# A hybrid mLSTM and SSD layer: side work of ScalarE and VectorE queued behind the latest bank copy and bank sum

## The chip, the cores and the metric

The kernel runs on one core of a Trainium2 chip, as one program. The metric is device time in microseconds (us). In what follows PE is TensorE (the matmuls), DVE is VectorE, ACT is ScalarE, POOL is GpSimd, and SP is the queue that issues the DMAs.

## What is computed

One decoder layer on 2048 tokens of width 1024, all in float32. The normalised stream is multiplied by one wide input matrix; its columns feed four mLSTM heads and two SSD groups, which run as recurrences over chunks of 128 tokens; both results are gated, normalised, and mapped back by an output matrix. Cut to what matters:

```python
h = rms_norm(x, norm_w[l])
proj = h @ w_in[l]                       # 2048 x 1024 by 1024 x 6680
q, k, v, i_pre, f_pre, o_pre, z_m, z_s, xbc, dt_raw = jnp.split(proj, SPLIT_POINTS, axis=-1)
hm = mlstm_chunkwise(q, k, v, log_i, log_f)          # 4 heads, chunks of 128
hm = norm(hm) * sigmoid(o_pre) * silu(z_m)
xs, Bm, Cm = split(silu(causal_depthwise_conv(xbc)))
y = ssd_chunked(xs, dt, A, Bm, Cm) + d_skip * xs     # 2 groups of 8 heads, chunks of 128
y = norm(y * silu(z_s))
x = x + concatenate([hm, y]) @ w_out[l]
return rms_norm(x, final_norm_w)
```

## The kernel before

**Products.** Both large matrix products are cut into 68 jobs. A job makes two blocks of 128 rows by 1024 columns by a Strassen-like scheme of seven products (`strassen`). One product is 12 matmuls of 128x512, because each operand is split into a high and a low float32r part (`split`: a cast on ACT, L191, and a difference on DVE, L192) and three of the four combinations are used. The left operands of a job are named L11, L12, S2, S3, S1, S4, L22, the right ones, which stay in SBUF for many jobs, R11, R21, T2, T3, T1, R22, T4. So a matmul `pj<-R22h,S4h` belongs to the sixth product of its job.

**Banks.** Products L11, S2, S1 and S4 add into the same PSUM bank `pa`, and between two of them ACT copies the bank out (*bank copy*: lines 276, 283, 289, and 302 or 327 for the last). The next product into the bank must wait for that copy. Two further banks are added to what was copied by DVE (*bank sum*: lines 280, 290, 296). Between the third copy (L289) and the product S4 only one product of the next job, L12, stands on PE. What a copy writes (`oa`, `ob`, `ca`, `cbt`) is one of four buffers, which comes free when the store of an earlier job's result (to `hd` or `gd`) has landed.

**Side work.** After each product `step` is called. It prepares the left operands of a coming job by one notch (`left`), and then lets other work go on by small pieces: the recurrences of a finished head or group (`rec_head`, `rec_group`, paced by `wv.to`), what they postponed (`later`, run by `tick`), the gates of a block of tokens (`gates`), and the operands of a later stage (`next_h`, `next_w`, called *prepared operands*: loads `xt`, `we`, `wg`, scalings in L511 and L533, splits `hqh`, `hql` in L396 and L398, and stores to DRAM). In a head's recurrence `scores` makes, for a chunk, `E` and `w` from a row `nmi` that a DMA loads (`w` in L690, `E` in L686 on DVE and L688 on ACT), then `kw`, `vt` and `st`; `memory` uses them on PE one turn later (L714 to L718).

**What sets the order.** PE runs its instructions in the order in which the program is written (`manual_schedule`). On the other engines and on SP a scheduler sets the order, when the kernel is built: it goes by its own reckoning of when an instruction can start, and lets one that seems to be ready pass another that was written earlier. On the chip each of these engines then works through its list in that order, and an instruction that waits holds all behind it.

Of the kernel before, what the change touches and what calls it, by code (L numbers as in the profile page):

```python
# [12 lines left out]
AF = mybir.ActivationFunctionType  # L13
# [56 lines left out]
def hybrid_layer(ctx, tc, x, norm_w, w_in, b_igate, b_fgate, conv_w, conv_b, dt_bias,  # L70
                 a_log, d_skip, mlstm_norm_w, ssd_norm_w, w_out, final_norm_w, out):
    nc = tc.nc
# [11 lines left out]
    def pj_tile():  # L84
        return psp.tile([P, TB], F32, tag="pj", name="pj")
# [8 lines left out]
    def ot(nm, n=1024):  # L94
        return mk([P, SUP + 16], "o", 4, nm)[:, 0:n]
# [4 lines left out]
    def tt_(nm):  # L100
        return mk([P, 1024], "t", 1, nm)
# [79 lines left out]
    def tick(n=1):  # L181
        clock[0] += n
        for t, fn in list(due):
            if t <= clock[0]:
                due.remove((t, fn))
                fn()
# [78 lines left out]
    def product(ps, L, R, start):  # L265
        lh, ll = L
        rh, rl = R
        for k in range(4):
            for n, (l, r) in enumerate(((lh, rh), (lh, rl), (ll, rh))):
                nc.tensor.matmul(ps, lhsT=l[:, k, :], rhs=r[:, k, :], start=start and k + n == 0,  # L270
                                 stop=k == 3 and n == 2, skip_group_check=True)

    def strassen(L, R, oa, ob, copy):
        pa = pj_tile()
        product(pa, L["L11"], R["R11"], True)
        nc.scalar.copy(oa[0], pa)  # L276
        yield
        ps = pj_tile()
        product(ps, L["L12"], R["R21"], True)
        nc.vector.tensor_add(oa[0], ps, oa[0])  # L280
        yield
        product(pa, L["S2"], R["T2"], False)
        nc.scalar.copy(ob[0], pa)  # L283
        yield
        pd = pj_tile()
        product(pd, L["S3"], R["T3"], True)
        yield
        product(pa, L["S1"], R["T1"], False)
        nc.scalar.copy(ob[1], pa)  # L289
        nc.vector.tensor_add(ob[1], pd, ob[1])  # L290
        yield
        product(pa, L["S4"], R["R22"], False)
        copy(oa[1], pa)
        yield
        product(pd, L["L22"], R["T4"], False)
        nc.vector.tensor_add(ob[0], pd, ob[0])

    def halves(t, o=0):
        return t[:, o:o + TB], t[:, o + TB:o + SUP]

    def evac_copy(dst, ps):
        nc.scalar.copy(dst, ps)

    def pair(L, R, s, ph, kind, j):
        n = int(ph[1])
        if kind == "conv":
            a, b = ot("ca", SUP + 3), ot("cbt", SUP + 3)
            yield from strassen(L, R, halves(a, 3), halves(b, 3), evac_copy)
            for i, raw in enumerate((a, b)):
                t = (8 + 2 * i + n) if j == 0 else n * 4 + j - 2 + i  # L310
                nc.scalar.copy(raw[:, 0:3], halo[:, t, :])
                nc.scalar.copy(halo[:, t, :], raw[:, SUP:SUP + 3])
                dst = tt_("cd")
                nc.scalar.activation(dst, raw[:, 0:SUP], AF.Identity, scale=cw[:, t, 0:1],
                                     bias=cb[:, t:t + 1])
                for q in range(1, 4):
                    nc.vector.scalar_tensor_tensor(dst, raw[:, q:q + SUP], cw[:, t, q:q + 1], dst,
                                                   op0=ALU.mult, op1=ALU.add)
                nc.scalar.activation(raw[:, 0:SUP], dst, AF.Tanh)
                nc.vector.scalar_tensor_tensor(raw[:, 0:SUP], raw[:, 0:SUP], 1.0, dst, op0=ALU.add, op1=ALU.mult)  # L320
                nc.sync.dma_start(gd[s][n][:, j + i, :], raw[:, 0:SUP])
            yield
            return
        a, b = ot("oa"), ot("ob")
        if kind == "oz":
            def first(dst, ps):
                nc.scalar.activation(dst, ps, AF.Tanh, scale=0.5)

            yield from strassen(L, R, halves(a), halves(b), first)
            nc.scalar.activation(a[:, 0:TB], a[:, 0:TB], AF.Tanh, scale=0.5)  # L330
            t = tt_("tz")
            nc.scalar.activation(t, b, AF.Tanh, scale=0.5)
            nc.vector.scalar_tensor_tensor(b, a, 1.0, b, op0=ALU.add, op1=ALU.mult)
            nc.vector.scalar_tensor_tensor(b, t, 1.0, b, op0=ALU.add, op1=ALU.mult)
            nc.sync.dma_start(hd[s][n][:, 4 + j, :], b)
        elif kind == "raw":
            yield from strassen(L, R, halves(a), halves(b), evac_copy)
            nc.sync.dma_start(hd[s][n][:, j, :], a)
            nc.sync.dma_start(hd[s][n][:, j + 1, :], b)
        else:  # L340
            yield from strassen(L, R, halves(a), halves(b), evac_copy)
            for i, z in enumerate((a, b)):
                t = tt_("tz")
                nc.scalar.activation(t, z, AF.Tanh, scale=0.5)
                nc.vector.scalar_tensor_tensor(z, t, 1.0, z, op0=ALU.add, op1=ALU.mult)
                nc.sync.dma_start(gd[s][n][:, j + i, :], z)
        yield
# [36 lines left out]
    def right_tile(o):  # L384
        return tuple(mk([P, 4, TB], o + k, 1, o + k, F32R) for k in "hl")

    def refill(o, d):
        rt = right_tile(o)
        for i in range(2):
            nc.sync.dma_start(rt[i].bitcast(F32), d[o][:, i])  # L390
        return rt
# [601 lines left out]
    def left():  # L993

        if ahead[0] < len(order):
            next(jobs[order[ahead[0]]]["left"])
            ahead[0] += 1
# [7 lines left out]
    def step(n, o):  # L1005

        left()
        if n + 1 < len(jobs) and jobs[n + 1]["new"]:
            st = jobs[n + 1]["stage"]
            Rs[st][o] = refill(o, refs[st])  # L1010
        tick()
        for t in [k for k in plan if k <= clock[0]]:
            for g in plan.pop(t):
                next(g, None)
        wv.to()
# [18 lines left out]
    for n, jb in enumerate(jobs):  # L1034
# [15 lines left out]
        if n == 0:  # L1050
            next(g)
            next(first)
            next(gm0)
            next(first)
            left()
            left()
            step(n, "R21")
        more = n + 1 < len(jobs)
        next(g)
        step(n, "T2")  # L1060
        next(g)
        step(n, "T3")
        if more:
            begin(n + 1)
# [51 lines left out]
```

## Time and profile before

| | |
|---|---|
| median of 3 runs | 1823.45 us |
| lowest and highest | 1819.24 and 1826.52 us |
| profiled execution, its own time | 1829.99 us |
| its span, first to last instruction | 1828.2 us |
| mean granted TensorE clock in it | 0.966 of full speed |
| busy: PE, DVE, ACT, POOL | 92%, 72%, 48%, 25% of the span |
| DMA packets' time, as a share of the 16 engines' span | 68.1% |

The span is what the trace shows; the 1.8 us around it are the launch's. Busy time is an average over stages that differ, and PE's is modelled: a matmul counts as busy until its result is drained, so matmuls overlap and a busy PE may still lose time to a lower clock. What PE loses is read from the gaps before its matmuls, and from what ended each gap.

### The profile page before, as it was taken

The page shows a single profiled execution, that of the slowest core. Times are in us where ns is not written, and L with a number is a line of the kernel's source. Part 1 is how long each engine was busy: PE and PEld are TensorE (multiplying, and loading weights), DVE is VectorE, ACT ScalarE, POOL GpSimd, SP SyncE. Part 2 cuts the span into 40 slices and gives each one's busy share as a digit, 9 for nine tenths or more (in the row PEclk, how much of TensorE's full clock was granted, in tenths as well). Part 3 has the DMA queues.
Part 4 walks back from the last instruction along what each step waited for, and adds up shares of the span by engine and source line. Part 5 has one row for each costly group of instructions (what it writes and reads, how often), then busy time and mean ns, then how long its engine had stood idle before and what let it go on. Part 6 is the DMA issues. An engine that isn't in the chain of part 4 may idle for free.

```text
span 1828.2 us, 25057 instructions
## 1 busy us (share of the span) xinstructions
PE 1679.5 (92%) x8072; PEld 1357.2 (74%) x8072; DVE 1308.7 (72%) x2417; ACT 880.6 (48%) x1880; POOL 450.2 (25%) x629
## 2 busy tenths in 40 slices
PE   4999999999899798989899999898988889997997
PEld 4688887778788685767788777777776667776885
DVE  7677968877567693888675895655678578864775
ACT  5344644456566663434564444655565433332443
POOL 2000413332122131223121331202211144532222
PEclk9999999999999899999999999999999989998999
DMA  5245666668787689655575658888877976678543
GB/s 153 93 156 174 185 212 203 207 212 256 224 258 231 181 274 379 206 182 179 161 203 185 196 181 272 290 278 263 258 260 250 384 260 212 205 265 315 189 158 115
DMA packets 358323, 405.32 MB, mean 222 GB/s; under 512 B 30224, under 2 KB 284432, under 8 KB 352816
## 3 DMA queue, kind: packets, MB, share of 16 engines
q1 hardware_dynamic: 358192, 403.72, 68.1%
q8 instruction: 64, 1.05, 0.2%
q14 instruction: 67, 0.55, 0.1%
HBM read 251.40 MB, written 152.24 MB: 221 GB/s over the span
## 4 chain that ended last, share of the span: by engine, by line
PE 25%; DMA 15%; DVE 7%; issue 3%; ACT 2%; SPq 1%; POOL 1%; DVEq 0%; POOLq 0%; ACTq 0%
PE pj L270 21%; DMA E<-arow 1%; DMA we<-in_w_out 1%; DVE E L798 1%; DMA nmi<-mrow 1%; DMA mx<-mix 1%; DMA gin<-gd 1%; DMA ws1R<-hqh 1%; DMA T4l<-ws1T 1%; DMA ws0T<-hql 1%; DMA ws0R<-hqh 1%; DMA ws0T<-hqh 1%; DMA xr<-in_x 1%; DMA ws1T<-hqh 1%; PE rc L872 1%
## 5 line engine op out<-in xcount | busy, mean ns | idle before, releaser
L733 POOL TENSOR_SCALAR sq<-dn,sq 128x1 f32<-128x1 f32 x64 | 46.1, 720 | 624.9 <-ACT sj L731 477.8
L270 PE MATMUL pj<-R22h,S4h 128*128 128x512 f32 x272 | 119.7, 440 | 38.1 <-ACT ob L289 24.6
L270 PE MATMUL pj<-T2h,S2h 128*128 128x512 f32 x272 | 113.4, 417 | 11.6 <-ACT ca L276 9.3
L270 PE MATMUL pj<-T1l,S1h 128*128 128x512 f32 x272 | 107.3, 395 | 7.6 <-DMA T1l<-ws1T 7.2
L270 PE MATMUL pj<-R22l,S4h 128*128 128x512 f32 x272 | 113.1, 416 | 0.0
L270 PE MATMUL pj<-T4h,L22h 128*128 128x512 f32 x272 | 111.5, 410 | 1.4 <-DMA T4h<-ws1T 1.4
L270 PE MATMUL pj<-R11h,L11h 128*128 128x512 f32 x272 | 112.7, 414 | 0.0
L270 PE MATMUL pj<-R22h,S4l 128*128 128x512 f32 x272 | 112.7, 414 | 0.0
L270 PE MATMUL pj<-T2l,S2h 128*128 128x512 f32 x272 | 109.0, 401 | 4.0 <-DMA T2l<-hsT 3.3
L270 PE MATMUL pj<-T1h,S1h 128*128 128x512 f32 x272 | 111.0, 408 | 1.4 <-ACT cbt L283 1.4
L270 PE MATMUL pj<-R21h,L12h 128*128 128x512 f32 x272 | 110.1, 405 | 0.0
L270 PE MATMUL pj<-T3h,S3h 128*128 128x512 f32 x272 | 109.3, 402 | 0.0
L270 PE MATMUL pj<-T2h,S2l 128*128 128x512 f32 x272 | 108.6, 399 | 0.0
L270 PE MATMUL pj<-T1h,S1l 128*128 128x512 f32 x272 | 107.2, 394 | 1.3 <-DVE S1l L192 1.3
L270 PE MATMUL pj<-T4l,L22h 128*128 128x512 f32 x272 | 106.6, 392 | 1.9 <-DMA T4l<-ws1T 1.9
L270 PE MATMUL pj<-T4h,L22l 128*128 128x512 f32 x272 | 106.7, 392 | 0.0
L270 PE MATMUL pj<-R11h,L11l 128*128 128x512 f32 x272 | 106.6, 392 | 0.0
L270 PE MATMUL pj<-R11l,L11h 128*128 128x512 f32 x272 | 106.5, 391 | 0.0
L270 PE MATMUL pj<-T3h,S3l 128*128 128x512 f32 x272 | 106.3, 391 | 0.0
L270 PE MATMUL pj<-R21l,L12h 128*128 128x512 f32 x272 | 106.3, 391 | 0.0
L270 PE MATMUL pj<-R21h,L12l 128*128 128x512 f32 x272 | 106.3, 391 | 0.0
L270 PE MATMUL pj<-T3l,S3h 128*128 128x512 f32 x272 | 106.3, 391 | 0.0
(330 smaller groups left out, 4697.4 us busy)
## 6 DMA issues: line engine op xcount, KB each, us to landing
wa<-in_w_in SPq DMA_DIRECT2D x52, 512.0 KB, 6.2
s<-sum SPq DMA_DIRECT2D x52, 512.0 KB, 5.3
hd<-ob SPq DMA_DIRECT2D x32, 512.0 KB, 3.8
E<-arow SPq DMA_DIRECT2D x32, 512.0 KB, 5.2
hin<-hd SPq DMA_DIRECT2D x64, 256.0 KB, 4.7
mx<-mix SPq DMA_DIRECT2D x32, 512.0 KB, 4.9
wb<-in_w_in SPq DMA_DIRECT2D x26, 512.0 KB, 4.2
sum<-ls SPq DMA_DIRECT2D x26, 512.0 KB, 4.6
```

Of the source, the lines that this page charges most:

```text
L270: nc.tensor.matmul(ps, lhsT=l[:, k, :], rhs=r[:, k, :], start=start and k + n == 0, stop=k == 3 and n == 2, skip_group_check=True)
L733: nc.gpsimd.tensor_scalar(sq, dn, DV * EPS, sq, op0=ALU.mult, op1=ALU.add)
L798: nc.vector.tensor_scalar(E[:, r, :], E[:, r, :], G["cum"][:, c, k:k + 1], 0.0, op0=ALU.subtract, op1=ALU.min)
L872: nc.tensor.matmul(yps[o:o + HD, (r // 2) * P:(r // 2 + 1) * P], lhsT=xdt[:, r * HD:(r + 1) * HD], rhs=E[:, r, :], start=True, stop=True, ...
```

## The change

A dictionary `tied` keeps the latest bank copy on ACT (`"a"`) and the latest bank sum on DVE (`"v"`), as the program is written. In `step`, all side work (`behind`: what `later` postponed, gates, prepared operands, recurrences) is written inside `tc.issue_after(...)` for both. For each instruction of that work on ACT this adds an edge for the scheduler from the latest bank copy, and for each on DVE one from the latest bank sum: it is queued behind them on its engine. The edges order the lists alone; they are no semaphore waits and add no instruction. The left operands (`left`) aren't tied. No instruction is added, removed or altered on any engine, and PE's order is the same.

```diff
+    tied = {}
+
+    def tie(k, i):
+        tied[k] = i.ins
+
     def strassen(L, R, oa, ob, copy):
         pa = pj_tile()
         product(pa, L["L11"], R["R11"], True)
-        nc.scalar.copy(oa[0], pa)
+        tie("a", nc.scalar.copy(oa[0], pa))
         yield
         ps = pj_tile()
         product(ps, L["L12"], R["R21"], True)
-        nc.vector.tensor_add(oa[0], ps, oa[0])
+        tie("v", nc.vector.tensor_add(oa[0], ps, oa[0]))
         yield
...
         product(pa, L["S1"], R["T1"], False)
-        nc.scalar.copy(ob[1], pa)
-        nc.vector.tensor_add(ob[1], pd, ob[1])
+        tie("a", nc.scalar.copy(ob[1], pa))
+        tie("v", nc.vector.tensor_add(ob[1], pd, ob[1]))
         yield
...
     def evac_copy(dst, ps):
-        nc.scalar.copy(dst, ps)
+        return nc.scalar.copy(dst, ps)
...
         if n + 1 < len(jobs) and jobs[n + 1]["new"]:
             st = jobs[n + 1]["stage"]
             Rs[st][o] = refill(o, refs[st])
+        with ExitStack() as es:
+            for i in tied.values():
+                es.enter_context(tc.issue_after(i))
+            behind()
+
+    def behind():
         tick()
         for t in [k for k in plan if k <= clock[0]]:
             for g in plan.pop(t):
```

Five lines are added ahead of `strassen`, so up to `step` a line number after the change is the number before plus 5: the bank copies L276, L283, L289 and L302 are L281, L288, L294 and L307, L396 is L401, L690 is L695.

**ACT's list, in the second half of the sequence, around the third bank copy of the job whose output is `ob_11173`.** `w_11580` and `w_11675` are rows of two coming chunks, `hqh_...` are splits of prepared operands. Before:

```order
L191 CAST S2h_11536<-s12_11190 128x512
L276 COPY oa_11489<-pj_11491 128x512
L396 CAST hqh_11545<-wg_11294 128x512
L690 ACTIVATE w_11675<-nmi_11487,u_8411 128x1
L191 CAST S3h_11565<-s34_11411 128x512
L289 COPY ob_11173<-pj_11174 128x512
```

and with the change:

```order
L191 CAST S2h_11536<-s12_11190 128x512
L281 COPY oa_11489<-pj_11491 128x512
L401 CAST hqh_11516<-we_11292 128x512
L191 CAST S3h_11565<-s34_11411 128x512
L294 COPY ob_11173<-pj_11174 128x512
L401 CAST hqh_11545<-wg_11294 128x512
L695 ACTIVATE w_11580<-nmi_11396,u_8411 128x1
```

`w_11675` leaves its place ahead of the copy (it now comes some fourteen places behind it), `hqh_11545` goes behind the copy, and the split of the prepared operand before that one, `hqh_11516`, moves in between the two copies.

**ACT's list, one phase later, around the third bank copy of the job with `ob_11770`.** `we_12050` and `wg_12052` are rows of the output matrix that are scaled after their load. Before:

```order
L276 COPY oa_12026<-pj_12028 128x512
L533 ACTIVATE we_12050<-we_12050,nwo_94 128x512
L191 CAST S3h_12099<-s34_11985 128x512
L533 ACTIVATE we_12050<-we_12050,nwo_94 128x512
L533 ACTIVATE wg_12052<-wg_12052,nwo_94 128x512
L289 COPY ob_11770<-pj_11771 128x512
```

and with the change:

```order
L281 COPY oa_12026<-pj_12028 128x512
L191 CAST S3h_12099<-s34_11985 128x512
L294 COPY ob_11770<-pj_11771 128x512
L538 ACTIVATE wg_12051<-wg_12051,nwo_94 128x512
L191 CAST L11h_12125<-wa_12042 128x512
L538 ACTIVATE we_12050<-we_12050,nwo_94 128x512
```

The three scalings that stood between the two copies have gone behind the second.

**ACT's list, in the first half of the sequence, where the conv jobs begin.** `E_6186`, `w_6189`, `kw_6200` and `vt_6202` belong to the first chunk that head 3 needs `memory` for. Before, they stand far ahead of the first bank copy of the conv job with `ca_6162`, which is row 631 of the list where `vt_6202` is row 604:

```order
L283 COPY cbt_5951<-pj_5952 128x512
L688 ACTIVATE E_6186<-E_6186,lns_87 128x128
L690 ACTIVATE w_6189<-nmi_6120,u_961 128x1
L690 ACTIVATE w_6321<-nmi_6124,u_961 128x1
L191 CAST L22h_6182<-wb_5706 128x512
L700 ACTIVATE kw_6200<-rc_6193,w_6189 128x128
L704 COPY vt_6202<-rc_6193 128x256
```

and with the change they stand behind it:

```order
L324 ACTIVATE ca_5688<-cd_6075 128x1024
L319 ACTIVATE cd_6085<-cbt_5689,cb_93,cw_92 128x1024
L281 COPY ca_6162<-pj_6164 128x512
L693 ACTIVATE E_6186<-E_6186,lns_87 128x128
L695 ACTIVATE w_6189<-nmi_6120,u_961 128x1
L695 ACTIVATE w_6321<-nmi_6124,u_961 128x1
L316 COPY ca_6162<-halo_96 128x3
L324 ACTIVATE cbt_5689<-cd_6085 128x1024
L705 ACTIVATE kw_6200<-rc_6193,w_6189 128x128
L709 COPY vt_6202<-rc_6193 128x256
```

All of what `memory` needs of this chunk has moved from ahead of the copy to `ca_6162` to behind it.

## Rows read from the trace of the kernel before

**Rows 1.** The page: busy us, share of the span and instructions by engine.

```profile
PE 1679.5 (92%) x8072; PEld 1357.2 (74%) x8072; DVE 1308.7 (72%) x2417; ACT 880.6 (48%) x1880; POOL 450.2 (25%) x629
```

**Rows 2.** Waits of PE: waiter <- releaser, us in total, times, longest.

```profile
PE pj L270 <- ACT ob L289: 24.6, 10, 5.9
PE pj L270 <- ACT cbt L289: 13.4, 5, 5.4
PE rc L813 <- DMA gin<-gd: 12.0, 1, 12.0
...
PE pj L270 <- ACT ca L276: 9.3, 1, 9.3
```

**Rows 3.** Waits of ACT, in the same columns.

```profile
ACT w L690 <- DMA nmi<-mrow: 91.7, 36, 5.5
...
ACT oa L276 <- DMA gd<-oa: 9.5, 3, 3.9
...
ACT ca L276 <- DMA gd<-ca: 6.1, 3, 3.4
```

**Rows 4.** Timeline (start, duration, instruction [idle before]) at `ob_11173`, ACT and PE.

```profile
1167.21 0.29 ACT L690 ACTIVATE w<-nmi,u 128x1 f32<-128x1 f32 x1 [3.77 <-DMA nmi<-mrow]
...
1168.55 0.80 PE L270 MATMUL pj<-R22h,S4h 128*128 128x512 f32 x1 [4.56 <-ACT ob L289]
```

**Rows 5.** Timeline at `ob_11770`, ACT and PE.

```profile
1216.84 0.72 ACT L533 ACTIVATE we<-we,nwo 128x512 f32<-128x512 f32 x1 [5.84 <-DMA we<-in_w_out]
...
1219.83 0.80 PE L270 MATMUL pj<-R22h,S4h 128*128 128x512 f32 x1 [4.37 <-ACT ob L289]
```

**Rows 6.** Timeline at the third copy of two jobs later, ACT and PE.

```profile
1274.03 0.30 ACT L690 ACTIVATE w<-nmi,u 128x1 f32<-128x1 f32 x1 [2.81 <-DMA nmi<-mrow]
...
1276.39 0.79 PE L270 MATMUL pj<-R22h,S4h 128*128 128x512 f32 x1 [5.12 <-ACT ob L289]
```

**Rows 7.** Timeline in head 2's recurrence, first half, ACT and PE.

```profile
477.33 0.30 ACT L690 ACTIVATE w<-nmi,u 128x1 f32<-128x1 f32 x1 [2.48 <-DMA nmi<-mrow]
479.95 0.30 ACT L690 ACTIVATE w<-nmi,u 128x1 f32<-128x1 f32 x1 [2.32 <-DMA nmi<-mrow]
...
493.57 0.80 PE L270 MATMUL pj<-R22h,S4h 128*128 128x512 f32 x1 [5.89 <-ACT ob L289]
```

**Rows 8.** Timeline at two conv jobs of the second half, ACT and PE.

```profile
897.17 0.29 ACT L690 ACTIVATE w<-nmi,u 128x1 f32<-128x1 f32 x1 [1.67 <-DMA nmi<-mrow]
...
899.57 0.79 PE L270 MATMUL pj<-R22h,S4h 128*128 128x512 f32 x1 [5.38 <-ACT cbt L289]
...
1314.27 0.30 ACT L690 ACTIVATE w<-nmi,u 128x1 f32<-128x1 f32 x1 [3.23 <-DMA nmi<-mrow]
...
1331.46 0.79 PE L270 MATMUL pj<-R22h,S4h 128*128 128x512 f32 x1 [4.45 <-ACT cbt L289]
```

**Rows 9.** Windows: us, busy (x instructions) by engine, granted clock, DMA share, GB/s.

```profile
1217.66:1224.49 6.83, 4.66 (x11) 3.69 (x12) 5.08 (x8) 4.08 (x8) 0.00 (x0) 0.50 0.81 272
...
1100.00:1450.00 350.00, 318.56 (x1427) 258.79 (x1425) 228.79 (x432) 196.64 (x434) 64.39 (x121) 0.96 0.83 279
```

**Rows 10.** Timeline: a bank copy and the use of the chunk tied to it.

```profile
1120.26 0.58 ACT L302 COPY oa<-pj 128x512 f32<-128x512 f32 x1
...
1124.10 0.60 PE L714 MATMUL rc<-vt,st 128*128 128x258 f32 x2
```

**Rows 11.** Timeline at `kw_6200` and `ca_6162`, ACT and PE.

```profile
610.52 0.37 ACT L700 ACTIVATE kw<-rc,w 128x128 f32<-128x128 f32 x1 [4.21 <-DVE st L698]
...
617.34 0.60 PE L714 MATMUL rc<-vt,st 128*128 128x258 f32 x2
...
630.48 0.59 ACT L276 COPY ca<-pj 128x512 f32<-128x512 f32 x1 [3.41 <-DMA gd<-ca]
...
631.11 0.80 PE L270 MATMUL pj<-T2h,S2h 128*128 128x512 f32 x1 [9.33 <-ACT ca L276]
...
633.08 1.06 ACT L319 ACTIVATE cbt<-cd 128x1024 f32<-128x1024 f32 x1 [1.92 <-DVE cd L317]
```

## What I predict

> **What bounds the kernel now.** I read the page's busy times first: PE is the busiest engine with 92% of the span, ACT has only 48% [rows 1]. So ACT's amount of work limits nothing; the question is what PE waits for in its gaps. The view of waits gives it: the largest cause is the third bank copy, L289, on which PE waits 24.6 + 13.4 = 38.0 us in 15 gaps; one more bank copy, L276 of a conv job, costs 9.3 us in a single gap, and one load, `gin`, 12.0 us [rows 2]. A copy takes about 0.6 us, so a gap of 5 us means that ACT came to it late. Six gaps hold 4.56 + 4.37 + 5.12 + 5.89 + 5.38 + 4.45 = 29.8 of the 38.0 us [rows 4 to 8].
>
> Next I asked what ACT did ahead of these copies. Its largest single wait is `w`, the row L690, for the load `nmi`: 91.7 us in 36 waits [rows 3]. In the gap at 1168.55 `w` stood between two bank copies and held ACT for 3.77 us [rows 4]; in that at 1219.83 it was a scaling of a prepared operand, L533, that waited 5.84 us for its load [rows 5]; at 1276.39 again `w`, 2.81 us [rows 6]. The waiting instruction isn't needed then. It only stands ahead of one that PE needs.
>
> A second loss follows from the first. After such a gap the granted clock is 0.50, the lower level of 1.2 GHz: from 1217.66 to 1224.49 PE ran 11 matmuls in 4.66 busy us, 0.42 us each, where over the whole phase it is 318.56 / 1427 = 0.22 us at a mean clock of 0.96 [rows 9]. So each matmul in such a stretch costs 0.20 us more. Six such stretches, one after each of the six gaps, hold 9 to 15 matmuls each (their windows read like the one shown).
>
> **The change, part by part.** It removes and adds nothing; PE's order stays. What moves is the place of side work in the lists of ACT, DVE and SP.
>
> *Side work goes behind the copies.* For the three gaps above the order shows the instruction that waited leaving its place ahead of the copy.
> - 1168.55: `w` waits 3.77 us and takes 0.29, the split ahead of it goes too, but an earlier split comes in. The copy could come up to 5 us sooner; the gap is 4.56 [rows 4], and I take all of it.
> - 1219.83: 5.84 us of wait and three scalings leave; the gap of 4.37 goes whole [rows 5].
> - 1276.39: `w` leaves with 2.81 us of wait and 0.30 of work: 3.1 of 5.12 [rows 6].
>
> That is 12.0 us. Three gaps are reached only through others' waits. At 493.57 two `w` held ACT 2.48 + 2.32 = 4.8 us ahead of the cast of S4; S4's difference frees the buffer for the next weights, these came late, and the cast of S2, waiting for their sum, held the copy [rows 7]. I take 3.5, between 0 and 4.8, near the upper end, since the chain is unbroken but eight scalings (L511) stay ahead of the copy. At 899.57 a `w` of 1.67 + 0.29 leaves: 1.9. At 1331.46 the copy stood behind a wait for an output buffer whose job had been held 3.23 us by `w`: 3.2, between 0 and 4.45 [rows 8]. Together 8.6. Of the other nine L289 gaps, 38.0 - 29.8 = 8.2 us, I take half, 4.
>
> *The clock.* The three gaps that go whole or nearly had 11, 11 and 15 matmuls in the slow stretches behind them: 37 x 0.20 = 7.4 us. The other three had 9, 10 and 13: 32 x 0.20 = 6.4, of which half. I take 10 us. The Trainium skill's page "TensorE: Matmul & The Clock Gate" (HAM oscillation) reckons such a loss as the throttled time times one half; by it the six stretches of 6.83 us would give up to 20 us and the sum below would be some 7 us better. The trace is kinder, since PE stood idle for part of each stretch.
>
> *What is queued behind a copy that isn't ready.* A copy also waits, for PE's product and for its output buffer. All side work written after it now stands behind it. For the heads I compared, for each of the 64 chunks, the end of the copy that `w` and `E` are now tied to with the start of the matmul that needs them (L714). In 63 cases it leaves 3.3 us or more; the tightest is a copy that ends at 1120.84 with L714 at 1124.10 [rows 10], and what must follow the copy (`E` 0.41, `kw` and `vt` 0.37 each, `st`) takes some 1.5 us. So nothing is late there: the chunk's turn, at least two products, covers it; without that cover each chunk would cost PE those 1.5 us.
>
> One case has no cover. The copy to `ca_6162` found its buffer only when a `gd` store had landed, at 630.48, some 25 us after its product; meanwhile ACT made `kw` at 610.52, and PE used it from 617.34 [rows 11]. Now `E`, `w`, `kw`, `vt` come after that copy. PE will stop at 617.34 instead of at 621.8 (631.11 less its gap of 9.33), and the 4.4 us of work between the two come after the wait, with 1.5 us of ACT work: 5.9 us lost if the copy ends as before. It may come sooner, as the 4.21 us that `kw` held ACT at 610.52 fall away: then 1.7. It may be later still, since a tanh of the conv (L319 before) stands ahead of `kw` too, and ended 3 us after the copy, at 634.14 [rows 11]: 9. I take 5.
>
> *DVE, POOL and SP.* DVE's moves are of the same work behind bank sums, and the waits of PE on DVE are small beside those on copies. SP's list changes with ACT's: splits made later store later, and stores wait in SP's list ahead of loads. I cost that at nothing, because `hin` and `nmi` are loaded two or three chunks ahead; without that cover a late `nmi`, up to 5.5 us a wait today [rows 3], would fall on PE.
>
> *Given back.* Between 1100 and 1450 the DMA engines are busy 0.83 of the time [rows 9]. If PE is faster there, loads must come faster; splits that wait for a store now stand between two copies. I let a third of the gain go: 12.0 + 8.6 + 4 + 10 = 34.6, less 11.5.
>
> **The sum.** 34.6 - 11.5 - 5 = 18.1 us. The profiled execution took 1829.99 us, 0.4% above the median of 1823.45; it falls to 1811.9, by 1.0%, and the median accordingly to **1805 us**. The bounds: with the three direct gaps alone, a third given back and 9 lost, 12.0 x 2/3 - 9, no gain; with nothing given back and 1.7 lost, 33 us.
>
> **The rivals.**
> - *The waits move on.* PE meets the next late load sooner and gives all back. For: the DMA share of 0.83, and a gap of 12.0 us that no copy causes [rows 2, 9]. Against: the waiting loads of these gaps are small ones of side work, and ACT often waits for PE to free operand buffers, so the left operands have slack. Time: 34.6 gained, some 30 given back, 5 lost: 1823.
> - *Late copies hold the recurrences.* Strict order works both ways: wherever a copy waits for its output buffer, PE now stops at the next recurrence. Price: 9 us at `ca_6162`, and the 9.5 + 6.1 us that such copies wait today [rows 3, 11] in full, 24.6 in all; it decides as soon as the gain that lasts is smaller than that. With a third of the gain, 11.5, left: 1823 + 13 = 1836, slower. Against it stand the 63 chunks with cover. The Trainium skill's page "PSUM — Partial Sum Buffer" (Engine vs sequencer instructions) says that the queues of ScalarE and VectorE are strict FIFO; the trace agrees, in that no later copy passed the `w` at 1167.21 [rows 4], and by that rule the side work can't pass a late copy either.
> - *More is freed.* Much of ACT's 91.7 us of waiting for `nmi` goes, operands are ready earlier throughout, and little is given back: 33 us or a little more, 1789.
> - That the change doesn't do what it says is no rival: all 64 `w` were ahead of the copy that they are now tied to.
>
> **How the numbers follow.** Forecast 0.55, waits move on 0.20, late copies 0.14, more freed 0.11. What a measurement can tell from no change is 0.5%, 9 us. Faster by more (below 1814): 0.11 and nine tenths of 0.55, with a little of the second, 0.63. Within: the second and the rest of the first, 0.22. Slower (above 1832.5): 0.15. The range of 8 in 10 reaches over the second rival to near the third, 1786 to 1833; cases of both signs hold the chance, and the forecast's own range is 1793 to 1815.
>
> **What would show it.** Right: PE's waits on L289 fall from 38 us to under 20; `w` on `nmi` from 91.7 to under 40; the half-clock stretches behind the gaps at 1168, 1219 and 1276 are gone; a new gap of 10 us or so before L714 in place of that at 631. Wrong: new gaps before L714 or L718 at more than one place; or L289's waits fall while those on loads of operands rise by as much.

## The result, and the profile after

The changed kernel takes 1845.73 us (median of 4 runs, 1838.38 to 1847.31), the kernel before beside it 1824.99 (4 runs, 1819.24 to 1827.18): a ratio of 1.0111, 95% interval 1.0074 to 1.0148. A second set of runs gave 1.0081 (1.0050 to 1.0112). The change makes the kernel about 1% slower; I had forecast 1% faster.

In the changed file a line number is five higher from `strassen` on (the third copy, L289, is L294; the first memory matmul, L714, is L719; the first matmul of `scores`, L694, is L699). The profiled execution took 1838.38 us, the fastest of its four, so its profile shows less than half of the loss. The second set's profile (1852.03 us, beside a median of 1851.9) stands beside it where the size matters.

The page's busy times, first the changed kernel, then its second profile:

```profile
PE 1679.8 (91%) x8072; PEld 1357.5 (74%) x8072; DVE 1305.0 (71%) x2417; ACT 877.0 (48%) x1880; POOL 445.6 (24%) x629
```

```profile
PE 1684.0 (91%) x8072; PEld 1359.8 (73%) x8072; DVE 1303.1 (70%) x2417; ACT 877.1 (47%) x1880; POOL 446.8 (24%) x629
```

No engine has more to do than before [rows 1]. The spans are 1828.2 before, 1836.7 and 1850.3 after, so the time in which PE is not busy grew from 1828.2 - 1679.5 = 148.7 us to 156.9 and 166.3. PE's waits, in the columns of [rows 2], the changed kernel and then its second profile:

```profile
PE rc L719 <- ACT vt L709: 17.5, 4, 12.4
PE rc L818 <- DMA gin<-gd: 12.9, 1, 12.9
...
PE pj L270 <- ACT ob L294: 10.6, 7, 3.8
PE rc L699 <- DVE C L728: 10.2, 5, 4.6
PE pj L270 <- ACT cbt L294: 9.8, 4, 3.9
...
PE rc L906 <- POOL dg L899: 7.5, 3, 3.5
```

```profile
PE rc L719 <- ACT vt L709: 16.0, 3, 12.1
PE rc L699 <- DVE C L728: 16.0, 6, 4.7
PE pj L270 <- ACT ob L294: 12.4, 7, 3.8
...
PE pj L270 <- ACT cbt L294: 11.0, 4, 3.6
...
PE rc L906 <- POOL dg L899: 9.1, 3, 4.7
```

The waits for the third bank copy fell from 24.6 + 13.4 = 38.0 us [rows 2] to 20.4 and 23.4, and the 9.3 us for the conv job's first copy are gone. So the change did what I said of the copies: 47.3 us became 20.4 and 23.4. But two waits of the heads' recurrences that weren't there before took as much back: `vt` (17.5, 16.0) and the state `C` (10.2, 16.0). Most of the rest of the growth is in the groups' recurrences, `dg` from 4.1 to 7.5 and 9.1 among them.

Two places show what the new waits are. The first is where I expected one, at `ca_6162`. Timeline of ACT there, and of PE:

```profile
623.48 0.59 ACT L281 COPY ca<-pj 128x512 f32<-128x512 f32 x1 [1.38 <-DMA gd<-ca]
...
626.15 1.06 ACT L324 ACTIVATE cbt<-cd 128x1024 f32<-128x1024 f32 x1 [1.34 <-DVE cd L322]
...
627.36 0.36 ACT L709 COPY vt<-rc 128x256 f32<-128x256 f32 x1
```

```profile
627.82 1.20 PE L719 MATMUL rc<-vt,st 128*128 128x258 f32 x2 [12.40 <-ACT vt L709]
```

The copy waits for its output buffer, `vt` now stands behind it and behind the tanh of the conv (L324), and PE stops at the memory matmul for 12.40 us instead of at the product for 9.33 [rows 11]. Set against the kernel before, matmul by matmul, PE lost 3.4 us between the chunk's first matmul at 614.61 and the products at 640 (3.6 in the second profile). A copy gap of 0.77 us just before that is gone; counted from ahead of it, the place cost 2.7 us (2.5).

The second I hadn't expected. Timelines of ACT, DVE and PE, in the changed kernel:

```profile
1256.52 0.58 ACT L307 COPY oa<-pj 128x512 f32<-128x512 f32 x1
...
1261.47 0.72 ACT L538 ACTIVATE we<-we,nwo 128x512 f32<-128x512 f32 x1 [4.17 <-DMA we<-in_w_out]
1262.22 0.62 ACT L401 CAST hqh<-we 128x512 fp32r<-128x512 f32 x1
```

```profile
1262.87 0.69 DVE L403 TENSOR_TENSOR hql<-we,hqh 128x512 fp32r<-128x512 f32 x1 [4.69 <-ACT hqh L401]
...
1265.25 0.48 DVE L728 SCALAR_TENSOR_TENSOR C<-C,nmi,rc 128x258 f32<-128x258 f32 x1
```

```profile
1265.78 0.69 PE L699 MATMUL rc<-hin 128*128 128x128 f32 x2 [4.65 <-DVE C L728]
```

A prepared operand's scaling waits 4.17 us for its load. Its split waits for it, and on DVE the split's second half waits for the first. Behind that, and behind a left operand's difference, stands `C`, which doesn't need any of them; PE waits for `C`, because the bank that it reads must be free for the next chunk. In the kernel before, the same operand was ready sooner (the `we` scaling at 1254.00 after 0.89 us of idle, its split on DVE at 1255.41, `C` at 1258.29), and PE passed the same matmul at 1258.84 without a gap:

```profile
1254.00 0.73 ACT L533 ACTIVATE we<-we,nwo 128x512 f32<-128x512 f32 x1 [0.89 <-DMA we<-in_w_out]
```

```profile
1258.29 0.48 DVE L723 SCALAR_TENSOR_TENSOR C<-C,nmi,rc 128x258 f32<-128x258 f32 x1
```

The load was issued at 1248.72 before and at 1256.21 now, each time 1.5 us behind the store of the split ahead of it (1247.24 and 1254.74): here the late split made the next load late. The second profile has the same chain: a split that waits 5.95 us, `C` behind it, and a gap of 4.72 us at 1271.60.

### The profile page after: what moved, and what is told of

Its sections match the earlier page's. It is cut to its first block, busy times and chain, and to the rows that moved or that the text cites. A ratio compares the mean times of both kernels' runs of the same rounds, so it can differ in the third digit from the quotient of the medians.

```text
span 1836.7 us, 25108 instructions
## 1 busy us (share of the span) xinstructions
PE 1679.8 (91%) x8072; PEld 1357.5 (74%) x8072; DVE 1305.0 (71%) x2417; ACT 877.0 (48%) x1880; POOL 445.6 (24%) x629
## 4 chain that ended last, share of the span: by engine, by line
PE 34%; DMA 18%; DVE 12%; issue 6%; ACT 3%; POOL 3%; SPq 2%; DVEq 0%; POOLq 0%; ACTq 0%
PE pj L270 27%; DMA E<-arow 2%; DMA ws0R<-hqh 1%; DMA xr<-in_x 1%; DVE cd L322 1%; DVE E L803 1%; DMA we<-in_w_out 1%; PE rc L877 1%; DMA z<-gd 1%; DMA T4l<-ws1T 1%; DMA gin<-gd 1%; DMA ws0T<-hqh 1%; PE rc L862 1%; DMA mx<-mix 1%; DVE hql L403 1%
## 5 line engine op out<-in xcount | busy, mean ns | idle before, releaser
L738 POOL TENSOR_SCALAR sq<-dn,sq 128x1 f32<-128x1 f32 x64 | 37.9, 591 | 674.8 <-ACT sj L736 495.4
```

The lines of the kernel that those rows point to most:

```text
L738: nc.gpsimd.tensor_scalar(sq, dn, DV * EPS, sq, op0=ALU.mult, op1=ALU.add)
```

## The experiments

Each is the kernel before with some of the ties of the change, or others; the code shown is cut from the difference to the changed kernel. The numbers behind a label are the ratio to the kernel before, measured beside it, and its 95% interval. "The half-clock time" is the sum of all stretches of the trace at a granted clock of 0.50: 127.9 us before, 132.4 and 135.6 after (some 2 us of each lie behind the last instruction).

**One engine at a time.** `e1_act` ties on ScalarE only, `e2_dve` on VectorE only:

```diff
-            for i in tied.values():
+            for i in [tied[k] for k in tied if k == "a"]:
```

> Side work is queued behind the latest bank copy on ScalarE alone; VectorE's side work is free again. Theory A (the loss comes from ScalarE: kw, vt and E stand behind a copy that waits for its output buffer, as at 627.82 where PE waits 12.4 us for vt): about as the changed kernel, 1840 to 1848, and the gap of 12.4 us stays. Theory B (the loss comes from VectorE: the state C, the scores and prepared operands stand behind a bank sum, PE waits 10.2 us for C): the L289 gain stays and C's waits go, 1825 to 1835. Theory C (prepared operands, set behind the same copy as the recurrences, hold them with their loads and stores): as the changed kernel or 5 us better.

> Side work is queued behind the latest bank sum on VectorE alone; ScalarE's is free again. Theory A: the wait at 617 for vt is gone, PE's waits for the third bank copy are back near 38 us: 1820 to 1830, no change from the kernel before. Theory B: worse than the kernel before by the new waits for C, about 10 us and their half-clock stretches: 1833 to 1842. Theory C: near the kernel before, within 8 us.

`e1_act`: 1.0046 (1.0029 to 1.0064). `vt` still costs PE 14.1 us, `C` 3.7. `e2_dve`: 1.0117 (1.0090 to 1.0144), as slow as the whole change, with no new single wait over 5 us. The waits for the third copy are 31.3 us, that for `C` is gone; the waits for `mx` (2.0 to 7.3), `q`, `xdt` and `dg` each grow by 2 to 5. The page of `e2_dve`:

```profile
PE 1692.0 (91%) x8072; PEld 1364.6 (74%) x8072; DVE 1302.5 (70%) x2417; ACT 878.5 (47%) x1880; POOL 451.8 (24%) x629
```

The same matmuls take 12.5 us longer than before [rows 1], and the half-clock time is 150.1; the other 9.3 us of its longer span are idle time of PE, in waits of 1.5 to 4.5 us at many places. So VectorE costs most (theory B), but not by `C`; and ScalarE's half, on which my gains rested, loses too.

**One kind of work at a time.** `e3_rec` ties only the recurrences (`tick` and `wv.to`), `e4_plan` only the planned work, gates and prepared operands, each on both engines:

```diff
+        with ExitStack() as es:
+            for i in tied.values():
+                es.enter_context(tc.issue_after(i))
+            wv.to()
```

> Only the recurrences (the heads' and groups' chunks and what they put off by some products) are queued behind copy and sum; gates and prepared operands are free again. Theories A and B (recurrences held by late copies or sums): at least as slow as the changed kernel, 1840 to 1850, with the gap before the memory matmul at 618 to 628 still there. Theory C (the prepared operands' loads and stores are what holds the recurrences): 1825 or faster, with the gaps at 1266 and 1355, where the scaling and the split of prepared operands stand ahead of E and C, gone.

> Only the gates and prepared operands are queued behind copy and sum; recurrences are free again. Theories A and B: the recurrence loss goes and part of the gain stays (the gap at 1220 where a scaling waited 5.8 us ahead of the copy): 1812 to 1822. Theory C: as slow as the changed kernel, 1838 to 1848, since the split and scaling still come late and in a bunch.

`e3_rec`: 1.0035 (1.0015 to 1.0054). `vt` 15.1 us, `C` 6.5, waits for the third copy 24.2. `e4_plan`: 1.0045 (1.0026 to 1.0064), with third-copy waits of 36.8, nothing gained. Neither theory is right alone: each kind loses about 0.4%, the gain at the copies comes from the recurrences' ties, and of these five kernels the wait for `C` is over 5 us only where the recurrences are tied on both engines.

**The tie one copy back.** `e5_prev` ties to the copy and sum before the latest, `e13_prev_act` and `e14_prev_dve` do so on one engine:

```diff
     def tie(k, i):
-        tied[k] = i.ins
+        if k in latest:
+            tied[k] = latest[k]
+        latest[k] = i.ins
```

> Side work is queued behind the last copy and sum but one, so that it may pass the one whose product is still running. Theory A+B (the loss is the recurrences that wait behind a copy or sum which isn't ready): PE's waits for vt and C (17.5 + 10.2 us in the changed kernel) fall under 8 us together, the waits for the third copy stay under 28: 1818 to 1828, equal to the kernel before or a little faster. Rival D (any tie, however early, disturbs the order of VectorE, POOL and the DMA queues in the group phases, as the order behind sums alone cost 1.2% without waits for vt or C): 1835 to 1845.

> All side work behind the last bank copy but one on ScalarE, VectorE free. Theory A: distance makes the loss, so no waits for vt or C over 6 us together, and, since VectorE's ties alone cost 1.2% at distance zero, this is the best of the kernels: 0.3 to 0.8% faster than the kernel before. Rival D (ScalarE's ties bunch the side work, at whatever distance): 0.2 to 0.6% slower.

> All side work behind the last bank sum but one on VectorE, ScalarE free. Behind the latest sum this half cost 1.2%, with no large wait of its own but 22 us more half-clock time. If distance makes the loss: within 0.4% of the kernel before, half-clock time 120 to 135 us. Rival D (VectorE's ties disturb the order of prepared operands and groups at any distance): 0.6 to 1.3% slower, half-clock time 140 us or more.

`e5_prev`: 0.9986 (0.9965 to 1.0006), against 1.0111 and 1.0081 at the latest copy. PE's waits for `vt` at the memory matmul fall to 0.4 us, for `C` to 3.6; those for the third copy are 26.9:

```profile
PE rc L703 <- DVE C L732: 3.6, 1, 3.6
...
PE rc L723 <- ACT vt L713: 0.4, 1, 0.4
```

`e13_prev_act`: 1.0008 (0.9990 to 1.0026), not faster as I expected, against 1.0046, and its waits for `vt` and `C` (6.3 and 4.4 us) are more than the 6 together that I expected. `e14_prev_dve`: 1.0024 (1.0004 to 1.0044), half-clock time 122.6, against 1.0117 and 150.1. On both engines it is the nearness of the copy that makes most of the loss. Tied one back, the work makes no gain that these intervals show.

**Recurrences on one engine.** `e6_rec_act` and `e16_rec_dve`:

```diff
+        with ExitStack() as es:
+            if "a" in tied:
+                es.enter_context(tc.issue_after(tied["a"]))
+            wv.to()
```

> Only the recurrences, and only their ScalarE instructions, are queued behind the latest bank copy. If the parts add (ScalarE's +0.46%, VectorE's +1.17%, recurrences +0.35%, prepared operands +0.45% against the kernel before), this is the cheapest quarter: 1815 to 1828 beside a kernel before at 1825 to 1830. Theory A (late copies alone make the loss): the gap near 628 stays and it is slower by 0.3 to 0.6%, as with recurrences on both engines.

> Recurrences alone, on VectorE alone, behind the latest bank sum. It splits the half that cost 1.2%. If it is the recurrences' small VectorE work (E, st, dn, y, xdt) that comes late behind sums: 1.008 to 1.013, waits for mx, q, xdt and vt raised as with all VectorE work tied, half-clock time 140 us or more. If it is the prepared operands' and gates' VectorE work: 1.000 to 1.005, half-clock time under 130.

1.0006 (0.9986 to 1.0027) and 1.0009 (0.9991 to 1.0027). In the first, `vt` costs 14.7 us and third-copy waits fall to 29.7: the exchange in small. In the second the half-clock time is 126.5. Both tie only `wv.to`; what `later` postponed, which `e3_rec` ties too, is free. So VectorE's 1.2% is not the paced part of its recurrences alone; the postponed part, and the prepared operands and gates on VectorE alone, were not tried.

The traces show one piece of that 1.2%. In the groups' recurrence of the first half the gates of a block of tokens, side work on DVE, come later. DVE, POOL and PE there, before and in `e2_dve`:

```profile
759.50 1.27 DVE L641 TENSOR_TENSOR_SCAN grow<-grow,mcar 4x512 f32<-4x512 f32 x1
...
771.55 1.04 POOL L849 TENSOR_TENSOR H<-H,cdec 128x512 f32<-128x512 f32 x1
...
773.06 0.38 PE L889 MATMUL rc<-ones,q 128*128 128x1 f32 x2 [0.69 <-POOL q L883]
```

```profile
775.58 1.26 DVE L646 TENSOR_TENSOR_SCAN grow<-grow,mcar 4x512 f32<-4x512 f32 x1
...
778.92 2.62 POOL L854 TENSOR_TENSOR H<-H,cdec 128x512 f32<-128x512 f32 x1
...
782.46 0.38 PE L894 MATMUL rc<-ones,q 128*128 128x1 f32 x2 [3.41 <-POOL q L888]
...
786.72 2.07 PE L862 MATMUL rc<-xw,bt 128*128 128x512 f32 x2 [3.55 <-DVE xdt L829]
```

The scan of the gates starts 6.9 us ahead of the matmul on `q` instead of 13.6, `H` and the first step of `z` ahead of `q` on POOL take 2.62 and 1.95 us instead of 1.04 each, and PE waits 3.4 us for `q` and some 3.5 more behind it. The same picture stands in every profile of a kernel that ties the planned work on VectorE to the latest sum (the change twice, `e2_dve`, `e4_plan`, `e8_noconv`) and in none of the others. Set against the kernel before, matmul by matmul from its 765 to its 835 us, PE loses 3 to 6 us there in these five profiles. The kernels that leave the left operands free and don't tie that work so lose 1.1 us at most.

**Only the instruction that I named.** `e7_w` ties `w` alone, on ScalarE; `e7_again` repeats it, `e12_w_prev` ties it one copy back, `e15_w_noconv` takes no copy of a conv job for a target:

```diff
+            with tc.issue_after(tied["a"]):
+                nc.scalar.activation(w, nmi[:, 0, P - 1:P], AF.Exp, bias=G["u"][:, c, h:h + 1])
```

> The kernel before, with one instruction of each head chunk, the factor w (the one that waited 91.7 us for its load), queued behind the latest bank copy; E, kw, vt and everything on VectorE are free. If w's wait ahead of the copies is what PE waits for: the waits for the third copy fall by 10 us or more and no wait for vt over 5 us appears: faster than the kernel before by 0.5 to 1%. If another instruction takes w's place ahead of the copy (the split, the scaling): waits for the third copy stay at 33 us or more and the time is unchanged.

> The run with w alone behind the latest copy, once more beside its variants. If its 0.3% was real: ratio 0.993 to 0.999, half-clock time under 115 us, gap of 10 to 12 us before the memory matmul near 622 again.

> w alone, behind the last bank copy but one. Theory A (what is tied to a copy that isn't ready stops PE at the recurrence): the gap of 11 us before the memory matmul near 622 goes, a gap of 5 to 9 us before the product at 631 is back, waits for the third copy stay at 30 to 36: as w behind the latest copy, or up to 0.3% better. If only the distance to the copy counts for the gain: w stands ahead of third copies again, waits near 38, no gain.

> w alone behind the latest bank copy of a job that isn't a convolution; behind a convolution's copies it is free. Theory A (the late copy of ca_6162 is what costs the version with w): the gap of 11 us near 622 before the memory matmul goes, one of 5 to 9 us before the product at 631 takes its place, waits for the third copy stay at 30 to 36: 0.2 to 0.5% faster than the kernel before, the fastest of the kernels. If the place of the gap doesn't matter to the sum: within 0.2% of the version with w behind every latest copy (0.9968 and 0.9985).

In this order: 0.9968 (0.9949 to 0.9986) and 0.9985 (0.9964 to 1.0006); 1.0004 (0.9983 to 1.0024); 0.9979 (0.9961 to 0.9998). The 91.7 us that `w` waited [rows 3] are gone from `e7_w`, yet PE's waits for the third copy are still 33.0 of 38.0 (34.1 in `e7_again`). ACT in `e7_w`, at the gaps of [rows 5] and [rows 6]:

```profile
1206.76 0.72 ACT L538 ACTIVATE we<-we,nwo 128x512 f32<-128x512 f32 x1 [7.36 <-DMA we<-in_w_out]
...
1209.13 0.56 ACT L294 COPY ob<-pj 128x512 f32<-128x512 f32 x1
...
1265.22 0.62 ACT L401 CAST hqh<-wg 128x512 fp32r<-128x512 f32 x1 [4.56 <-issue]
...
1266.26 0.58 ACT L294 COPY ob<-pj 128x512 f32<-128x512 f32 x1
```

Another instruction that comes late stands ahead of the copy: at the first place the scaling, which waits for its load as before, at the second a split, for whose 4.56 us the profile names no releaser. The gaps are 6.09 and 6.02 us instead of 4.37 and 5.12. One copy back (`e12_w_prev`), `w` waits 5.7 us again, the third copies cost 30.9, and the gap at 631 is back with 8.9 us. With conv copies spared, the gap before the memory matmul goes, one of 9.3 before the product comes back, and the time is the same within the intervals: its place doesn't matter to the sum. `w` alone behind the latest copy, conv copies spared or not, comes out ahead of the kernel before by 0.15% to 0.3%, in two of the three measurements by more than the interval; no other version does.

**Conv copies spared in the whole change.** `e8_noconv` (a conv job passes `keep=False`; `e15_w_noconv` has the same edit):

```diff
-    def strassen(L, R, oa, ob, copy):
+    def strassen(L, R, oa, ob, copy, keep=True):
+        def tie(k, i):
+            if keep:
+                tied[k] = i.ins
```

> The changed kernel, but copies and sums of the convolution jobs are no targets: behind those, side work is queued only behind the last copy of another job. Theory A (a copy late for its output buffer, ca_6162, holds the chunk): the gap of 12.4 us before the memory matmul is gone, a gap of some 9 us before the product at 631 is back, and the time is 3 to 6 us better than the changed kernel's. Rival D: within 3 us of the changed kernel.

1.0059 (1.0040 to 1.0079), better than the change by 0.2 to 0.5%, though the intervals meet. A gap of 8.9 us is back before the product in place of the 12.4; `C` still costs 12.3.

**What then stood ahead of the copies.** In the changed kernel, timeline of ACT at the gap of [rows 5], 3.83 us now:

```profile
1220.65 0.62 ACT L191 CAST S3h<-s 128x512 fp32r<-128x512 f32 x1 [3.30 <-DMA s<-sum]
1221.18 0.58 ACT L294 COPY ob<-pj 128x512 f32<-128x512 f32 x1
```

It is a split of a coming left operand, which the change doesn't tie. So `e9_left` ties these splits alone, `e10_w_left` these and `w`, `e11_w_left_plan` the planned work too, all on ScalarE:

```diff
-        left()
+        with tc.issue_after(tied["a"]):
+            left()
```

> The kernel before, with only the splits of left operands on ScalarE (the work of left(), which the change leaves free) queued behind the latest bank copy; w, recurrences and prepared operands are free. Theory E (what holds the third copy is whatever load-bound cast stands ahead of it; with w gone it was the cast of S3 at 1220, 1267 and 1323): the waits for the third copy fall below 28 us, the gap at 1331 goes, those at 1168 and 1276, with a w ahead, stay: 1822 to 1830, or 0 to 0.4% faster. Rival F (the cast holds the copy since the operand itself is late, and PE would meet it a product later): waits for S3h and S4h on PE appear, time unchanged or slower.

> w and the splits of left operands behind the latest bank copy on ScalarE, all else free. Theory E: waits for the third copy fall to 20 us or less, only gaps with a scaling or a split of a prepared operand ahead (1210, 1267) stay; half-clock time at or under the 99 us of w alone; 0.5 to 0.9% faster than the kernel before. Rival F: as w alone, 0.3% faster, or slower.

> As the run with w and left operands, with gates and prepared operands on ScalarE behind the copy too. Theory E: nothing load-bound is left ahead of the third copy, its waits fall to 12 us or less: 0.6 to 1.1% faster. If the prepared operands' own bunching costs (they alone on both engines gave 0.45% slower): no better than w and left operands without them, or back at the kernel before.

1.0221 (1.0196 to 1.0247), 1.0154 (1.0124 to 1.0185), 1.0158 (1.0134 to 1.0183): slower, as rival F has it, and clearly, but not by its sign, since no wait for S3h or S4h appears. The waits of `e9_left`:

```profile
PE pj L270 <- ACT ob L294: 21.0, 11, 6.4
PE rc L877 <- DVE y L907: 14.1, 8, 2.9
PE pj L270 <- ACT cbt L294: 12.7, 5, 4.4
...
PE pj L270 <- ACT L22h L191: 11.4, 1, 11.4
```

PE now waits 11.4 us for an operand, and 14.1 instead of 3.9 us for the groups' `y`, while the third copies still cost 33.7. The wait of 11.4 us is at `ca_6162` once more: the cast of L22h, tied to that copy, starts at 636.77, right behind it (636.29, 0.59 us). So this shows an operand made late by the tie rather than one that comes late by itself.

**The change once more.**

> The changed kernel once more, beside the kernel before and the following runs on one chip, for a ratio that can be set beside theirs and a second profile. If the places of the loss are real and not of one execution: the gap of 12 us before the memory matmul near 628, waits for C of 8 us or more between 1130 and 1300, and waits for the third copy of 17 to 24 us are all there again; ratio 1.008 to 1.014.

All of it is there again, with a ratio of 1.0081; its other numbers stand in the first section.

## Why the prediction was wrong

The result is nearest to the rival "late copies hold the recurrences" (1836 us, chance 0.14), and has something of "the waits move on". Its time is 10 us above that rival's, and late copies of conv jobs, sparing which gives back 0.2 to 0.5% of the 0.8 to 1.1% (`e8_noconv`), are the smaller part of the loss. Step by step:

- *Side work goes behind the copies.* The direction was right and the size nearly: the forecast was under 20 us of waits on the third copy, and they are 20.4 and 23.4. Of the three gaps that I took as direct, those at 1168 and 1276 are gone; that at 1220 is 3.83 instead of 4.37, because a split of a left operand had waited behind the scaling and now waits for its own load. `w` on `nmi`, forecast under 40, has no wait left.
- *That `w` was the cause* did not hold. By itself it is worth 4 to 5 of the 38 us of third-copy waits. The scaling of prepared operands (`we`) waited 11.4 us before and waits 22.6 in `e7_w`: the next late instruction in ACT's list takes up the time that `w` gives free.
- *What is queued behind a copy that isn't ready* is **the step that failed**: "So nothing is late there: the chunk's turn, at least two products, covers it". Outside `ca_6162` the sum had no term for it; the new waits of the heads there (`vt` and `C` without the one at `ca_6162`) are 17.5 + 10.2 - 12.4 = 15.3 us, and 19.9 in the second profile. I had measured the slack from the tied copy to L714 [rows 10], on ACT alone, with every other instruction at its old time. But not only `w` and `E` are tied to the copy: the scalings and splits of prepared operands are, too, and with them comes a load. At 1265.78 the copy was on time; what held the chunk was the 4.17 us of a load that stood behind the copy and ahead of the chunk. And the chunk has more exits than L714: `C` on DVE holds L699.
- *The one case with no cover*, `ca_6162`, was right: a gap of 12.40 us before the memory matmul in place of 9.33, forecast 10. The cost, taken as 5, is 3.4 and 3.6 from the chunk's first matmul on (2.7 and 2.5 with the small copy gap ahead of it), within the bounds 1.7 to 9. The tanh that I put into the upper bound did come ahead of `kw`, but the copy came 7 us sooner than before.
- *DVE, POOL and SP* failed with it. DVE's moves got no term at all, and of SP's list I wrote "I cost that at nothing". VectorE's ties alone cost 1.2% (`e2_dve`), some 21 us and the dearest single part. My cover was that `hin` and `nmi` are loaded early, and PE has no wait for them. What comes late is the loads of prepared operands and, in the groups' recurrence, the gates on DVE, with two waits of some 3.4 us in place of two under 1 us.
- *The clock*: 10 us forecast as gained, nothing came. Two of the three slow stretches are gone, but new gaps have their own (one from 617.39 to 631.04, others from 1265.92 and 1354.67), and the sum went from 127.9 to 132.4 and 135.6. What failed is the number of slow stretches. Their price was nearly right: 69 matmuls at 0.20 us in six stretches of 6.83 make 0.34 us per slow microsecond, and a straight line through PE's busy time and the half-clock time of the 20 profiles has a slope of 0.42, without the three kernels that tie left operands 0.36. These kernels differ in other ways as well, so it is a rough figure. The Trainium skill's page "TensorE: Matmul & The Clock Gate" (HAM oscillation) reckons half; the trace agrees roughly, with the slope of 0.36 to 0.42 somewhat below it, and here the slope counts.
- *Given back*: a third was taken, but all and more came back. Copies gave 47.3 - 20.4 = 26.9 us (23.9 in the second profile); `vt` and `C` took 27.7 (32.0).

Of the signs that I named for being wrong, the first came: new gaps before L714 at two places, 627.82 and 1354.81.

That the recurrences wait because of what they are queued behind is shown: tied one copy and one sum further back (`e5_prev`), `vt`'s gaps at the memory matmul go, `C` falls to 3.6 us, and the loss goes with them. That it was the late copy at `ca_6162` is shown by `e8_noconv`. The gap there isn't most of the loss, for without it 0.6% are left. The Trainium skill's page "PSUM — Partial Sum Buffer" (Engine vs sequencer instructions) calls these queues strict FIFO. The trace agrees: `C` started only after the split that had waited 4.69 us. How the whole of VectorE's 1.2% splits is not settled: the gates' place accounts for 3 to 6 us of some 21. The parts don't add: 0.46% and 1.17% for the engines make 0.8 to 1.1% together, and the paced recurrences alone on VectorE cost 0.1% (0.9991 to 1.0027, so perhaps nothing).

## What to carry to other kernels

A tie to the latest product's copy forbids the wrong order at one place and can make a new one elsewhere: the work that was ready during the product now comes in a bunch after it, and at 1265.78 its load-bound parts stood ahead of the part that PE needed next. Before one queues work behind an instruction, the slack to be measured is that of the whole bunch, on every engine, with the loads that it brings, and not that of one instruction at its old time. And where an engine that isn't the bottleneck waits for many loads, removing the largest of these waits (91.7 us here) is worth only what PE then waits less. PE's waits for the third copy fell by 4 to 5 us, and all of its idle time from 148.7 us to 148.4 and 146.2.

## What the hardware showed

One instruction per chunk is enough to move a gap: with `w` alone behind the late conv copy PE stops 10.7 us at the memory matmul, with that copy spared 9.3 us at the product behind it, and the whole time is the same within the intervals. A loss can come without any large new wait: in `e2_dve` the same 8072 matmuls took 12.5 us longer, with 27 stretches at the lower clock level instead of 21 and 22 us more of half-clock time. By the slope of 0.36 to 0.42 that is 8 to 9 of the 12.5 us, an estimate. And work that moves on one engine can lengthen another's: the same step `H` on POOL took 1.04 us in the kernel before and 2.62 where the gates on DVE had come next to it. Why it did is not shown.
